# The last sixteen rows of a sum of reciprocals on one order list

## The chip, the cores and the metric

The kernel runs on one core of a Trainium2 chip. The metric is the device time of one execution in microseconds. The kernel before takes 172.44 us, the median of 12 runs (171.76 to 172.76).

## The reference

For x of 32 x 512 x 1024 float32, all positive, the output is the sum of 1/x over the last axis:

```python
def setup_inputs():
    batch, seq, dim = 32, 512, 1024
    return {"x": np.abs(np.random.randn(batch, seq, dim)).astype(np.float32) + 1e-6}

def reference(x):
    return np.sum(1.0 / x, axis=-1).astype(np.float32)
```

## The kernel before

The 16,384 sums are spread over 128 partitions, so each partition holds 128 rows ("row c" below is row c of all partitions at once) of 1024 elements. A ring of 40 rows in SBUF takes the loads; all are issued in row order on SP's queue (L124), eleven of 8 rows, six of 4 rows and eight of 2 rows. A load waits until the earlier users of its ring slots are done, and for the landing of the load eight before it, whose semaphore it takes.

Each row is cut into halves a and b of 512, and the kernel computes only one reciprocal for each pair of elements, in three steps:

- **Product** p = a * b. GpSimd (POOL) makes most of them (L143), two rows in one instruction where it can. For one row in a chunk of kind C, TensorE copies b to PSUM by a matmul with the identity (`add` into the tile `b`, L131) and VectorE multiplies a by it (L132).
- **Reciprocal** 1/p = exp(-ln p) on ScalarE (ACT): Ln in place with a scale of 2^17 (L154), then Exp with scale -1. For a chunk of kind A, Exp writes to a PSUM tile `r` (L162); for B and C it writes in place (L169).
- **Sum** on VectorE (DVE), `sum_row` (L93 to L104), which multiplies, and reduces to one column of `sums`. In a chunk of kind A each element of the row is multiplied by its r (a * 1/(ab) = 1/b, b * 1/(ab) = 1/a), 1024 elements. In B and C TensorE has added a + b into a PSUM tile `s` (L149, L150), and VectorE multiplies 512 elements of 1/p by s. Each sum is followed by a short read of the accumulator.

`LOADS` (L42 to L44) lists the chunks of two rows. The last sixteen rows, 112 to 127, are eight loads of one chunk each: A, B, A, C, A, B, A, C. In the last four rows (`SINGLE`, L34) Exp goes row by row, and the rest goes in pairs. The sums of a chunk are issued one chunk late (`waiting`, L152 and L170), so that VectorE doesn't stand before ScalarE.

Every engine works through its instructions in the program's order (`keep`). Tiles come from pools that rotate: four buffers for each of the two kinds of product tiles, three banks for s, one for b, two tiles of two banks for r. An instruction that takes a buffer waits until its former users are done.

Of the kernel before, what the change touches and what calls it, by code (L numbers as in the profile page):

```python
# [1 line left out]

# [6 lines left out]


@with_exitstack
def kernel(
    ctx: ExitStack,
    tc: tile.TileContext,
    x: bass.AP,
    out: bass.AP,
):

    nc = tc.nc
    f32 = mybir.dt.float32
    P = 128  # L30
    D = 1024
    H = D // 2
    F = 128
    SINGLE = 124  # L34

    R = 40

    S = float(2**17)

    A, B, C = (2, 0, 0), (2, 2, 0), (2, 2, 1)  # L42
    LOADS = [[A, B, A, B], [A, B, A, C]] * 5 + [[A, B, A, C]]
    LOADS += [[A, B], [A, C]] * 3 + [[A], [B], [A], [C]] * 2  # L44

    Ln = mybir.ActivationFunctionType.Ln
    Exp = mybir.ActivationFunctionType.Exp
    mult = mybir.AluOpType.mult
    plus = mybir.AluOpType.add

    x_v = x.flatten_outer_dims().rearrange("(p f) d -> p f d", p=P)
    out_v = out.flatten().rearrange("(p f) -> p f", p=P)

    act_sets = list(get_activation_tables(nc.m.arch).keys())
    nc.scalar.add_instruction(  # L55
        mybir.InstLoadActFuncSet(
            name=nc.get_next_instruction_name(),
            act_func_set_id=act_sets.index("natural_log_exp_and_others"),
            ins=[],
            outs=[],  # L60
        )
    )

    ppool = ctx.enter_context(tc.tile_pool(name="ppool", bufs=4))
    opool = ctx.enter_context(tc.tile_pool(name="opool", bufs=1))
    spool = ctx.enter_context(
        tc.tile_pool(name="spool", bufs=3, space=bass.MemoryType.PSUM)
    )
    bpool = ctx.enter_context(
        tc.tile_pool(name="bpool", bufs=1, space=bass.MemoryType.PSUM)  # L70
    )
    rpool = ctx.enter_context(
        tc.tile_pool(name="rpool", bufs=2, space=bass.MemoryType.PSUM)
    )

    ring = opool.tile([P, R, D], f32)
    sums = opool.tile([P, F], f32)
    ident = opool.tile([P, P], f32)
    make_identity(nc, ident)
    keep = tc.keep_in_program_order  # L80

    def add(bank, *halves):
        for k, half in enumerate(halves):
            i = nc.tensor.matmul(  # L84
                bank,
                lhsT=ident,
                rhs=half,
                start=k == 0,
                stop=k == len(halves) - 1,
            )  # L90
            keep(i)

    def sum_row(c, row, fac, out=None):  # L93
        i = nc.vector.tensor_tensor_reduce(  # L94
            out=row if out is None else out,
            in0=row,
            in1=fac,
            scale=S,
            scalar=0.0,
            op0=mult,  # L100
            op1=plus,
            accum_out=sums[:, c : c + 1],
        )
        keep(i)  # L104

    def sum_rows(c, xc, pr, sm, rc):
        m, e = xc.shape[1], len(sm)
        for j in range(e, m):
            row = xc[:, j, :].rearrange("p (h e) -> p h e", h=2)
            sum_row(  # L110
                c + j,
                row,
                rc[j - e].unsqueeze(1).to_broadcast([P, 2, H]),
                pr[:, e : e + 2, :] if j == e and e + 1 < m and c < SINGLE else None,
            )
        for j in reversed(range(e)):
            sum_row(c + j, pr[:, j, :], sm[j])

    waiting = None
    c0 = 0  # L120
    for chunks in LOADS:
        n = sum(m for m, _, _ in chunks)
        xt = ring[:, c0 % R : c0 % R + n, :]
        keep(nc.sync.dma_start(out=xt, in_=x_v[:, c0 : c0 + n, :]))  # L124

        made, q = [], 0
        for m, e, v in chunks:
            pr = ppool.tile([P, m, H], f32, tag="ps" if e else "pr")
            for j in range(v):
                b = bpool.tile([P, H], f32, tag="b")  # L130
                add(b, xt[:, q + j, H:])  # L131
                i = nc.vector.tensor_tensor(  # L132
                    out=pr[:, j, :], in0=xt[:, q + j, :H], in1=b, op=mult
                )
                keep(i)
            made.append(pr)
            q += m

        q = 0
        for (m, e, v), pr in zip(chunks, made):  # L140
            xc = xt[:, q : q + m, :]
            if v < m:
                i = nc.gpsimd.tensor_tensor(  # L143
                    out=pr[:, v:, :], in0=xc[:, v:, :H], in1=xc[:, v:, H:], op=mult
                )
                keep(i)
            sm = []
            for j in range(e):
                s = spool.tile([P, H], f32, tag="s")  # L149
                add(s, xc[:, j, :H], xc[:, j, H:])  # L150
                sm.append(s)
            if waiting:  # L152
                sum_rows(*waiting)
            keep(nc.scalar.activation(out=pr, in_=pr, func=Ln, scale=S))  # L154

            step = 1 if c0 + q >= SINGLE else m
            rc = []
            for j in range(e, m, step):
                to = min(j + step, m)
                r = rpool.tile([P, to - j, H], f32, tag="rc")  # L160
                keep(
                    nc.scalar.activation(  # L162
                        out=r, in_=pr[:, j:to, :], func=Exp, scale=-1.0
                    )
                )
                rc += [r[:, l, :] for l in range(to - j)]
            for to in range(e, 0, -step):
                r = pr[:, max(to - step, 0) : to, :]
                keep(nc.scalar.activation(out=r, in_=r, func=Exp, scale=-1.0))  # L169
            waiting = c0 + q, xc, pr, sm, rc  # L170
            q += m
        c0 += n
    assert c0 == F, c0
    sum_rows(*waiting)

    nc.sync.dma_start(out=out_v, in_=sums)


# [1 line left out]
_INS = ['x']  # L180
_OUTS = [((32, 512), 'float32')]


# [23 lines left out]
```

## Time and profile before

| | us |
|---|---|
| median of 12 runs | 172.44 |
| the profiled execution, its own time | 172.69 |
| its span, first to last instruction | 170.9 |
| POOL busy | 138.4 (81%) |
| ACT busy | 134.3 (79%) |
| PE busy | 131.6 (77%) |
| DVE busy | 122.4 (72%) |
| DMA, mean rate over the span | 393 GB/s |

The span runs from the first instruction to the last one of the profiled execution; the device time is a little more. The chain of work that ended last is found backwards from the last instruction: at each step to what released it. All times below that have a place ("at 161.95") are us from the start of the span. In the groups of instructions, the columns are the line, the engine, the operation, its output and inputs by tile name, partitions x elements, the count, and after the bar the busy time and mean duration in ns, and after the second bar the idle time ahead of them and what ended it. The granted TensorE clock is 0.999.

### The profile page before, as it was taken

To read this page: it belongs to the slowest core of one execution; us is meant where nothing else is said; L and a number is where in the kernel's file an instruction comes from. 1 tells how busy PE (TensorE), PEld (TensorE's weight loads), DVE (VectorE), ACT (ScalarE), POOL (GpSimd) and SP (SyncE) were. 2 spreads that over 40 slices of the span, in tenths; PEclk is the share of its full clock that TensorE was granted. 3 is DMA by queue.
4 is the path that set the end of the run, shared out by engine and by line. 5 is a ranking of instruction groups with operands and counts; after the bars stand their busy time and mean duration, and the time that the engine had idled before them with its cause. 6 is when DMAs were issued, how large, how long until landed. Compare 5 with 4: busy or idle time off the path is not lost.

```text
span 170.9 us, 1264 instructions
## 1 busy us (share of the span) xinstructions
PE 131.6 (77%) x278; PEld 50.1 (29%) x278; DVE 122.4 (72%) x267; ACT 134.3 (79%) x131; POOL 138.4 (81%) x70
## 2 busy tenths in 40 slices
PE   0008999594978879785988869788899999988790
PEld 0003333241322333232333323233243343333230
DVE  0000877748977677778777677888789898889783
ACT  3003979959797988978889787888999998998890
POOL 1008999499996999699996989989999999997920
PEclk9999999999999999999999999999999999999999
DMA  6999999899999999999999999999999999999400
GB/s 215 414 460 414 453 414 453 368 430 430 430 431 422 453 407 464 384 431 437 422 445 422 445 422 431 399 430 424 430 430 430 430 408 418 422 418 424 169 0 15
DMA packets 3751, 67.24 MB, mean 393 GB/s; under 512 B 417, under 2 KB 545, under 8 KB 545
## 3 DMA queue, kind: packets, MB, share of 16 engines
q1 hardware_dynamic: 3744, 67.18, 92.8%
q8 instruction: 2, 0.03, 0.1%
q14 instruction: 5, 0.03, 0.0%
HBM read 67.11 MB, written 0.07 MB: 393 GB/s over the span
## 4 chain that ended last, share of the span: by engine, by line
DMA 80%; POOL 7%; issue 3%; PE 3%; ACT 3%; DVE 2%; SPq 1%; DVEq 0%; POOLq 0%
DMA ring<-in_x_dram 80%; POOL pr L143 7%; PE s L84 2%; ACT pr L154 2%; DVE ring L94 1%; SPq L124 1%; DVE pr L94 1%; PE b L84 1%; ACT r L162 1%; DVEq L202 0%; ACT pr L169 0%; DVE sums L94 0%; POOLq L143 0%; DVEq L94 0%
## 5 line engine op out<-in xcount | busy, mean ns | idle before, releaser
L143 POOL TENSOR_TENSOR pr<-ring 128x1024 f32<-128x1024 f32 x64 | 137.7, 2184 | 24.4 <-DMA ring<-in_x_dram 24.1
L84 PE MATMUL s<-ring,ident 128*128 128x512 f32 x256 | 122.1, 613 | 32.9 <-DVE sums L94 16.9
L154 ACT ACTIVATE pr<-pr 128x1024 f32<-128x1024 f32 x64 | 67.4, 1053 | 29.3 <-POOL pr L143 29.2
L84 PEld LDWEIGHTS s<-ring,ident 128*128 128x128 f32 x256 | 46.5, 192 | 105.9 <-issue 62.5
L94 DVE CUSTOM_DVE_ANT_1 pr<-ring,r 128x1024 f32<-128x1024 f32 x31 | 37.9, 1221 | 44.9 <-ACT r L162 44.9
L94 DVE CUSTOM_DVE_ANT_0 pr<-pr,s 128x512 f32<-128x512 f32 x64 | 41.3, 683 | 0.7 <-PE s L84 0.5
L94 DVE CUSTOM_DVE_ANT_1 ring<-ring,r 128x1024 f32<-128x1024 f32 x33 | 40.1, 1216 | 0.0
L169 ACT ACTIVATE pr<-pr 128x1024 f32<-128x1024 f32 (+1 forms) x33 | 33.9, 1031 | 1.0
L162 ACT ACTIVATE r<-pr 128x1024 f32<-128x1024 f32 (+1 forms) x33 | 33.0, 1001 | 1.0
L84 PE MATMUL b<-ring,ident 128*128 128x512 f32 x22 | 12.0, 626 | 2.1 <-DMA ring<-in_x_dram 2.0
L94 DVE DVE_READ_ACCUMULATOR2_ANT sums<- 128x1 f32 x128 | 10.5, 82 | 0.0
L132 DVE TENSOR_TENSOR pr<-ring,b 128x512 f32<-128x512 f32 x11 | 7.5, 682 | 0.1
L84 PEld LDWEIGHTS b<-ring,ident 128*128 128x128 f32 x22 | 3.6, 188 | 9.7 <-DMA ring<-in_x_dram 8.3
L55 ACT ACT_TABLE_LOAD x1 | 1.3, 1283 | 0.7 <-PEq L191 0.7
masks.py:197 POOL MEMSET ident<- 128x128 f32 x1 | 0.2, 204 | 0.3 <-POOLq L191 0.3
masks.py:199 POOL TENSOR_SCALAR_AFFINE_SELECT ident<-ident 128x128 f32<-128x128 f32 x1 | 0.3, 292 | 0.1
L191 POOL MEMSET const-float32-0.0<- 128x1 f32 x1 | 0.1, 98 | 0.2 <-issue 0.2
L191 POOL MEMSET const-bfloat16-1.0<- 128x1 bf16 x1 | 0.1, 101 | 0.0
L191 POOL MEMSET const-uint8-127<- 128x1 uint8 x1 | 0.1, 101 | 0.0
L191 POOL MEMSET const-float32-1.0<- 128x1 f32 x1 | 0.1, 98 | 0.0
## 6 DMA issues: line engine op xcount, KB each, us to landing
ring<-in_x_dram SPq DMA_DIRECT2D x11, 4096.0 KB, 37.0
ring<-in_x_dram SPq DMA_DIRECT2D x6, 2048.0 KB, 37.3
ring<-in_x_dram SPq DMA_DIRECT2D x8, 1024.0 KB, 28.8
out_dram<-sums SPq DMA_DIRECT2D x1, 64.0 KB, 1.6
```

The costliest lines, as they stand in the source:

```text
L55: nc.scalar.add_instruction(mybir.InstLoadActFuncSet(name=nc.get_next_instruction_name(), act_func_set_id=act_sets.index("natural_log_exp_ ...
L84: i = nc.tensor.matmul(bank, lhsT=ident, rhs=half, start=k == 0, stop=k == len(halves) - 1,)
L94: i = nc.vector.tensor_tensor_reduce(out=row if out is None else out, in0=row, in1=fac, scale=S, scalar=0.0, op0=mult, op1=plus, accum_out ...
L124: keep(nc.sync.dma_start(out=xt, in_=x_v[:, c0 : c0 + n, :]))
L132: i = nc.vector.tensor_tensor(out=pr[:, j, :], in0=xt[:, q + j, :H], in1=b, op=mult)
L143: i = nc.gpsimd.tensor_tensor(out=pr[:, v:, :], in0=xc[:, v:, :H], in1=xc[:, v:, H:], op=mult)
L154: keep(nc.scalar.activation(out=pr, in_=pr, func=Ln, scale=S))
L162: nc.scalar.activation(out=r, in_=pr[:, j:to, :], func=Exp, scale=-1.0)
L169: keep(nc.scalar.activation(out=r, in_=r, func=Exp, scale=-1.0))
L191: nc = _bacc.Bacc("TRN2", target_bir_lowering=False, num_devices=1)
```

## The change

Rows 0 to 111 stay as they are. The chunks of the last sixteen rows leave `LOADS` (and `SINGLE` goes); their loads become six of two rows and four of one row. All their operations are written in one list, `ORDER`, and a new loop issues them as they stand there, so that each engine gets its share in that order. A letter is an operation, the number its row, and "+" means that it covers this row and the next:

- P: product on GpSimd. D: product on VectorE with both inputs in SBUF. B and V: TensorE copies b to PSUM, and VectorE multiplies by it.
- S: TensorE adds a + b into a tile s. L: Ln. E: Exp, in place for rows that have an S, else into a tile r. T: the sum on VectorE.
- W and X: row 124 goes another way: Ln over all 1024 elements of the row in place, then Exp with scale -1 and the sum over the row from ScalarE's accumulator straight into `sums`. This row has no product, no s and no work on VectorE.

VectorE's products are rows 117 (V) and 121 (D) where they were 118 and 126. The rows summed against s are 115, 118, 119, 122, 123, 126 and 127, where they were 114, 115, 118, 119, 122, 123, 126 and 127. Rows 125, 126 and 127 go through product, Ln, Exp and sum row by row. The store of `sums` now waits for ScalarE as well as for VectorE.

```diff
-    SINGLE = 124
...
-    LOADS += [[A, B], [A, C]] * 3 + [[A], [B], [A], [C]] * 2
+    LOADS += [[A, B], [A, C]] * 3
+    LAST = 112
+    LAST_LOADS = [2] * 6 + [1] * 4
+    ORDER = """
+        P112+ P114+ L112+ B117 E112+ P116 S115 V117 L114+ T113 L116+ P118 S118
+        T112 E114 E115 P119 T114 E116+ S119 P120 L118+ T115 D121 E118+ T117
+        L120+ S122 P122+ T116 E120+ T119 W124 T118 P125 L122+ T120 S123 P126
+        L125 T121 E122+ S126 P127 E125 T122 L126 T123 L127 S127 T125 E126 E127
+        T126 X124 T127
+    """
...
+    c0 = LAST
+    for n in LAST_LOADS:
+        xt = ring[:, c0 % R : c0 % R + n, :]
+        keep(nc.sync.dma_start(out=xt, in_=x_v[:, c0 : c0 + n, :]))
+        c0 += n
     assert c0 == F, c0
     sum_rows(*waiting)
+
+    prs, rs, ss, bs = {}, {}, {}, {}
+    order = ORDER.split()
+    added = {int(op[1:]) for op in order if op[0] == "S"}
+    dead = set()
+
+    def pair(c):
+        k = (c - LAST) // 2
+        if k not in prs:
+            pr = ppool.tile([P, 2, H], f32, tag=("pr", "ps")[k % 2])
+            prs[k] = pr
+        return prs[k]
+
+    for op in order:
+        kind, c, n = op[0], int(op[1:].rstrip("+")), 1 + op.endswith("+")
+        j = (c - LAST) % 2
+        rows = ring[:, c % R : c % R + n, :]
+        a, b = rows[:, :, :H], rows[:, :, H:]
+        pr = None if kind in "WX" else pair(c)[:, j : j + n, :]
+        if kind == "P":
+            keep(nc.gpsimd.tensor_tensor(out=pr, in0=a, in1=b, op=mult))
+        elif kind == "D":
+            keep(nc.vector.tensor_tensor(out=pr, in0=a, in1=b, op=mult))
+        elif kind == "B":
+            bb = bpool.tile([P, H], f32, tag="b")
+            add(bb, b[:, 0, :])
+            bs[c] = bb
+        elif kind == "V":
+            keep(
+                nc.vector.tensor_tensor(
+                    out=pr[:, 0, :], in0=a[:, 0, :], in1=bs[c], op=mult
+                )
+            )
+        elif kind == "S":
+            s = spool.tile([P, H], f32, tag="s")
+            add(s, a[:, 0, :], b[:, 0, :])
+            ss[c] = s
+        elif kind == "L":
+            keep(nc.scalar.activation(out=pr, in_=pr, func=Ln, scale=S))
+        elif kind == "E":
+            r = pr
+            if c not in added:
+                r = rpool.tile([P, n, H], f32, tag="rc")
+                rs.update({c + l: r[:, l, :] for l in range(n)})
+            keep(nc.scalar.activation(out=r, in_=pr, func=Exp, scale=-1.0))
+            if n == 2:
+                dead.add((c - LAST) // 2)
+        elif kind == "T" and c in added:
+            sum_row(c, pr[:, 0, :], ss[c])
+        elif kind == "T":
+            row = rows[:, 0, :].rearrange("p (h e) -> p h e", h=2)
+            k = (c - LAST) // 2
+            to = prs[k] if k in dead else None
+            dead.discard(k)
+            sum_row(c, row, rs[c].unsqueeze(1).to_broadcast([P, 2, H]), to)
+        elif kind == "W":
+            keep(nc.scalar.activation(out=rows, in_=rows, func=Ln))
+        elif kind == "X":
+            keep(
+                nc.scalar.activation(
+                    out=rows,
+                    in_=rows,
+                    func=Exp,
+                    scale=-1.0,
+                    accum_out=sums[:, c : c + 1],
+                )
+            )
 
     nc.sync.dma_start(out=out_v, in_=sums)
```

## The prediction

> **What bounds the kernel now.** I read the page's chain of work first, then that chain in order of time for the last 30 us, then the busy time by stretch, then the groups by shape of the last 24 us. The chain, as start us, us, what:
>
> ```profile
> 104.02 37.55 DMA ring<-in_x_dram
> ...
> 141.65 20.30 DMA ring<-in_x_dram
> 161.95 0.04 issue
> 161.99 1.13 PE b L84 x2
> 163.12 3.45 PE s L84 x8
> ...
> 167.40 0.60 DVE pr L94
> 168.00 0.01 DVE sums L94
> ```
>
> Until 161.95 the chain is loads and nothing else (the page gives them 80% of the span). From the last landing to the last sum it takes 168.01 - 161.95 = 6.06 us. In that tail it is not ScalarE but TensorE that is late: two b matmuls for row 126, then eight s matmuls for rows 126 and 127 in a row, and VectorE's last two sums behind them. After that come 2.9 us for the store and the end of the program (168.01 to 170.9), and 172.69 - 170.9 = 1.79 us outside the span. Only the tail of 6.06 us is open to an edit of the last rows.
>
> The stretches, each with us, busy time (count) of PE, PEld, DVE, ACT, POOL, then clock, DMA share, GB/s:
>
> ```profile
> 148.00:157.00 9.00, 7.72 (x17) 2.69 (x15) 8.48 (x20) 8.48 (x9) 7.87 (x4) 1.00 1.01 422
> 157.00:162.00 5.00, 3.68 (x9) 1.44 (x9) 3.82 (x9) 4.20 (x4) 4.78 (x3) 1.00 0.56 234
> 162.00:168.00 6.00, 4.55 (x10) 1.81 (x10) 5.41 (x13) 4.30 (x6) 1.29 (x2) 1.00 0.00 0
> ```
>
> The DMA engines are full to 157 and then run out unevenly. VectorE and ScalarE have 0.5 us of slack each in nine at 148 to 157, so a tail that gives ScalarE more work must find it there or after 157. In the tail VectorE is busy for 5.41 of 6.0 us.
>
> Prices of the tail's shapes (busy us, mean ns):
>
> ```profile
> L143 POOL TENSOR_TENSOR pr<-ring 128x1024 f32<-128x1024 f32 x6 | 14.2, 2379 | 1.4 <-DMA ring<-in_x_dram 1.1
> L154 ACT ACTIVATE pr<-pr 128x1024 f32<-128x1024 f32 x10 | 10.5, 1051 | 1.6 <-POOL pr L143 1.5 <-DVE pr L132 0.2
> L94 DVE CUSTOM_DVE_ANT_0 pr<-pr,s 128x512 f32<-128x512 f32 x12 | 7.8, 683 | 0.7 <-PE s L84 0.5 <-ACT pr L169 0.2
> L94 DVE CUSTOM_DVE_ANT_1 ring<-ring,r 128x1024 f32<-128x1024 f32 x6 | 7.2, 1216 | 0.0
> L162 ACT ACTIVATE r<-pr 128x1024 f32<-128x1024 f32 x4 | 4.1, 1028 | 0.1
> L143 POOL TENSOR_TENSOR pr<-ring 128x512 f32<-128x512 f32 x3 | 3.9, 1285 | 0.1
> L132 DVE TENSOR_TENSOR pr<-ring,b 128x512 f32<-128x512 f32 x2 | 1.4, 684 | 0.1
> L162 ACT ACTIVATE r<-pr 128x512 f32<-128x512 f32 x2 | 1.1, 592 | 0.0
> ```
>
> Queued, they follow each other closer than their means: in the trace POOL 2.33 and 1.24 us, ACT 0.97 (two rows) and 0.54 (one row), but 1.07 where an Exp waits for the Ln just before it; VectorE 1.14 (sum against r) and 0.61 (sum against s); TensorE 0.43 per matmul, so 1.72 per row of s. Hand-overs cost 0.03 us from POOL to ACT and from ACT to VectorE, 0.16 from TensorE's last matmul to VectorE (166.55 to 166.71).
>
> [...] The trace has 684 for L132. I take 0.69 for D121.
> [...]
>
> **The change part by part.** Up to row 111 every engine's order is the same. I take the state at hand-over from the trace: POOL free at 145.28, ScalarE ready for the Ln of rows 112-113 at 148.21, VectorE done with row 110 at 149.78. Loads land (last of 16 completions) at 144.60, 147.09, 149.57, 152.05, 154.54 and 157.02 for pairs 112 to 122, then 159.51 and 161.95 today.
>
> *Loads.* Two loads of two rows become four of one, in the same place of SP's queue. SP issues the last load today at 141.65, 20 us ahead of its landing; the new last one waits for rows 114-115 to land (147.09), still some 15 us ahead, so the queue doesn't run dry. A packet per partition took 1213, 614 and 312 ns at 32, 16 and 8 KB: by doubling, 10 to 15 ns of each are fixed. At 4 KB that is (312 + 10) / 2, some 160 ns (estimate), by eight per DMA engine 1.28 us a row. Rows land at 158.30, 159.58, 160.86 and 162.14: the last 0.2 later, the others sooner. Lower bound 1.24 a row (no fixed part), upper 1.5.
>
> *TensorE.* Removed: b of 118 and 126 and s of 114; added: b of 117, which stands ahead of S115 in its queue (S115 then runs 150.51 to 152.39, wanted at 154.79). Seven rows of s are left where there were eight. S127 needs the bank of row 122: T122 ends at 163.31, S127 runs 163.42 to 165.40. This replaces 166.55, a gain of 1.15 on the chain that ends last today.
>
> *POOL.* Six pairs and two single rows become three pairs (P112, P114, P122) and seven single rows: 118 and 126 come to POOL, 117, 121 and 124 leave it. A single row costs 1.24, half a pair 1.17. From 152.16: P118 to 153.44, P119 154.68, P120 155.93, P122 (landing 157.02) 157.13 to 159.51, P125 160.97, P126 162.25, P127 163.53 (today 163.39).
>
> *VectorE.* V117 waits for b (landing 149.57, two matmuls to 150.74): 150.77 to 151.45. T113, T112 to 153.73; T114, T115 to 155.48; D121 is ready at 155.41[...]: to 156.62. Behind it T117, T116, T119, T118, T120, T121 to 162.41; T122 to 163.31, T123, T125, T126 to 165.67, T127 from 165.59 (S127 ready 165.40 + 0.16, E127 at 165.28) to 166.28. In all one sum against s is gone (eight to seven; the eight against r stay, row 114's for row 124's), 0.61 less.
>
> *ScalarE.* 14 two-row and 4 one-row operations become 11 two-row and 8 one-row ones and W124 and X124: from 14 x 1.0 + 4 x 0.54 = 16.2 to 13 x 1.0 + 8 x 0.54 = 17.3, and the accumulator read. So it works longer, but nothing of VectorE has to follow its last instruction. By start: L112 148.21, E112 149.29, L114 150.25, L116 151.48 (0.25 idle for V117), E114 152.46, E115 153.00, E116 153.79 (0.25 idle: its r bank is free after T112), L118 154.76, E118 155.84, L120 156.80 (D121 done 156.62), E120 157.88, W124 158.84, L122 159.83 (P122 done 159.51), L125 161.00 (P125 done 160.97), E122 161.55, E125 162.51, L126 163.05, L127 163.59 (P127 done 163.53), E126 164.14, E127 164.67, X124 165.21. X124 takes 1.05, and then reads out its accumulator. No row here prices that read on ScalarE: it can't be below 0, and I bound it above by a whole 512-wide ACTIVATE, 0.6; I take 0.2, between VectorE's own read of 0.08 and that bound. It ends at 166.46.
>
> *Sum.* The last work ends at 166.46 (ScalarE; VectorE 166.28) in place of 168.01: 1.55 us less. The store now waits for ScalarE as well; the 2.9 us behind it stay. Against the profiled execution: 172.69 - 1.55 = 171.14. The median of the runs stands 0.25 below that execution: **170.9 us**.
>
> With the bounds: accumulator read 0 to 0.6 gives 166.28 to 166.86; 1.24 to 1.35 us a row gives 166.38 to 166.71; ScalarE 1.0 late at hand-over gives 166.75, VectorE 1.0 late gives no change. So 170.7 to 171.3 on the median, with 0.2 either way for the sampling.
>
> **The rivals.**
> - *The tail is landing-bound after all.* L127 starts when P127 is done, and my ScalarE queue reaches it only 0.03 later, so a later landing moves the end by its full size. At 1.5 us a row, row 127 lands at 163.02, the end is 167.31, the time 171.75. For it: row loads halve the packet, and the DMA engines end unevenly today. Against it: halving from 16 to 8 KB cost only some 2%.
> - *Slower: D121 misses its window.* POOL is idle only from 155.93 to 157.13, when P122 begins. If VectorE comes to D121 after 157.13[...] it waits until 159.51 and ends at 160.20. L120 then starts at 160.23 in place of 156.80, everything behind it on ScalarE follows without a gap, and X124 ends at 169.70: 1.69 later than today, 174.1. It decides from a delay of D121 of 1.7 us.[...] Against: VectorE's queue ahead of D121 is set by landings 5 us earlier.
> - *No change.* Several small new waits (E116 on T112, L116 on V117, S127 on T122) each 0.4 longer than drawn would bring the end to 166.46 + 1.2 = 167.7, 172.1. For it: all three stand in in-order queues, so what is behind waits too. Against: ScalarE makes up delays of its start to 1.0 us almost in full before L125, where POOL sets its time.
>
> **How the numbers follow.** Forecast (ScalarE's queue sets the end, 170.6 to 171.4): 0.68. Landing-bound (171.4 to 172.0): 0.18. No change (172.1 to 172.8): 0.08. Slower (D121): 0.06. About 0.2% is what a measurement of this kernel can tell from no change. Faster by over that: 0.68 + 0.18 = 0.86; within: 0.08; slower: 0.06. The range takes the forecast with its bounds and most of the landing case: 170.4 to 171.8.
>
> **What would show it.** Right: the chain's last pieces are ScalarE's X124 or VectorE's T127 near 166.4, no row of TensorE after 165.6, D121 within 155.4 to 156.7, ScalarE without a gap over 0.3 us from 148.2 on, POOL's last product ending near 163.5. Wrong: a wait of L120 for VectorE, P127 starting after 162.6, an accumulator read on ScalarE over 0.6, or main rows whose landings differ from today's by over 0.3.

## The result and the profile after

The changed kernel takes 170.43 us, the median of 11 runs (170.04 to 170.95), against 172.31 us for the kernel before, measured beside it. The ratio is 0.9894, 95% interval 0.9878 to 0.9910, so some 1.8 us or 1.1% faster (1.55 to 2.1 us). A second measurement gave 0.9893 (e10). The prediction was 170.9 us against 172.44, 1.55 us faster, with a range of 170.4 to 171.8.

The chain of work that ended last, in order of time, of the changed kernel (start us, us, what):

```profile
141.55 18.02 DMA ring<-in_x_dram
...
159.72 1.29 POOL pr L211
...
161.57 1.05 ACT pr L235
162.62 0.02 issue
162.64 0.50 DVE pr L108
...
163.94 1.13 DVE ring L108
...
165.69 0.60 DVE pr L108
166.29 0.01 DVE sums L108
```

The chain leaves the loads at 159.58, not at 161.95: what it follows is no longer the last landing but row 125's, whose product GpSimd makes at once. TensorE is gone from it; the two long pieces of s and b matmuls that closed the chain before have no successor here. The last work ends at 166.30 where it ended at 168.01. The span is 169.0 us.

The same stretches as before (us, then busy us and count of PE, PEld, DVE, ACT, POOL, clock, DMA share, GB/s):

```profile
148.00:157.00 9.00, 6.28 (x14) 2.52 (x14) 8.02 (x17) 8.42 (x11) 6.88 (x5) 1.00 1.00 413
157.00:162.00 5.00, 4.53 (x10) 1.92 (x11) 5.00 (x11) 4.77 (x6) 4.66 (x3) 1.00 0.61 242
162.00:168.00 6.00, 3.11 (x7) 0.87 (x5) 3.92 (x12) 4.25 (x8) 1.48 (x2) 1.00 0.04 11
```

From 157 to 162 VectorE is now busy all the time (5.00 of 5.00, before 3.82) and ScalarE nearly so (4.77, before 4.20). Work that used to come after 162 now runs before it: after 162 VectorE has 3.92 us left in place of 5.41, TensorE 3.11 in place of 4.55.

ScalarE from L120 on, where the predicted schedule can be held against it line by line:

```profile
156.81 1.04 ACT L229 ACTIVATE pr<-pr 128x1024 f32<-128x1024 f32 x1
157.88 1.03 ACT L235 ACTIVATE r<-pr 128x1024 f32<-128x1024 f32 x1
158.84 1.04 ACT L247 ACTIVATE ring<-ring 128x1024 f32<-128x1024 f32 x1
159.79 1.04 ACT L229 ACTIVATE pr<-pr 128x1024 f32<-128x1024 f32 x1
161.03 0.63 ACT L229 ACTIVATE pr<-pr 128x512 f32<-128x512 f32 x1 [0.20 <-POOL pr L211]
161.57 1.04 ACT L235 ACTIVATE pr<-pr 128x1024 f32<-128x1024 f32 x1
162.51 0.58 ACT L235 ACTIVATE r<-pr 128x512 f32<-128x512 f32 x1
163.03 1.13 ACT L229 ACTIVATE pr<-pr 128x512 f32<-128x512 f32 x2
164.07 1.13 ACT L235 ACTIVATE pr<-pr 128x512 f32<-128x512 f32 x2
165.11 1.04 ACT L250 ACTIVATE ring<-ring 128x1024 f32<-128x1024 f32 x1
166.06 0.19 ACT L250 ACTIVATION_READ_ACCUMULATOR ring<-ring 128x1 f32 x1
```

These are L120, E120, W124, L122, L125 (0.20 idle for GpSimd's product of row 125), E122, E125, L126 and L127, E126 and E127, X124 and its accumulator read. No start is more than 0.1 us from the predicted one.

Landings move from one profiled execution to the next by up to 1 us: GpSimd's product of rows 122 and 123, which follows their landing, starts at 157.18 in both kernels and at 156.19 in e8. So below I give for each kernel, beside the ratio, the time from the start of that product to the end of the last work. I call it the tail time. It is 168.01 - 157.18 = 10.83 us in the kernel before and 166.30 - 157.18 = 9.12 us in the changed one: 1.71 less.

### The profile page after: what moved, and what is told of

Same layout as the page of the kernel before. It is cut to its first block, busy times and chain, and to the rows that moved or that the text cites. A ratio compares the mean times of both kernels' runs of the same rounds, so it can differ in the third digit from the quotient of the medians.

```text
span 169.0 us, 1264 instructions
## 1 busy us (share of the span) xinstructions
PE 130.6 (77%) x272; PEld 50.2 (30%) x272; DVE 121.8 (72%) x265; ACT 134.7 (80%) x135; POOL 137.5 (81%) x72
## 4 chain that ended last, share of the span: by engine, by line
DMA 79%; POOL 8%; issue 4%; DVE 3%; ACT 3%; SPq 1%; POOLq 0%; DVEq 0%
DMA ring<-in_x_dram 79%; POOL pr L157 7%; DVE ring L108 2%; ACT pr L168 2%; DVE pr L108 1%; POOL pr L211 1%; SPq L138 1%; ACT r L173 1%; ACT pr L235 1%; DVE sums L108 0%; ACT pr L178 0%; POOLq L157 0%; DVEq L285 0%; POOLq L211 0%; ACT pr L229 0%
## 5 line engine op out<-in xcount | busy, mean ns | idle before, releaser
L157 POOL TENSOR_TENSOR pr<-ring 128x1024 f32<-128x1024 f32 (+1 forms) x56 | 121.1, 2198 | 22.9 <-DMA ring<-in_x_dram 22.9
L168 ACT ACTIVATE pr<-pr 128x1024 f32<-128x1024 f32 x56 | 59.0, 1053 | 28.2 <-POOL pr L157 28.2
L178 ACT ACTIVATE pr<-pr 128x1024 f32<-128x1024 f32 x28 | 29.6, 1058 | 0.9
L173 ACT ACTIVATE r<-pr 128x1024 f32<-128x1024 f32 x28 | 28.8, 1028 | 0.9
L211 POOL TENSOR_TENSOR pr<-ring 128x512 f32<-128x512 f32 (+1 forms) x10 | 15.8, 1605 | 2.5 <-DMA ring<-in_x_dram 2.5
L98 PE MATMUL b<-ring,ident 128*128 128x512 f32 x18 | 9.6, 616 | 0.3 <-DMA ring<-in_x_dram 0.3
L229 ACT ACTIVATE pr<-pr 128x1024 f32<-128x1024 f32 (+1 forms) x9 | 8.0, 902 | 0.5 <-DVE pr L220 0.3
L146 DVE TENSOR_TENSOR pr<-ring,b 128x512 f32<-128x512 f32 x9 | 6.2, 683 | 0.6 <-PE b L98 0.6
L235 ACT ACTIVATE r<-pr 128x1024 f32<-128x1024 f32 (+1 forms) x5 | 4.2, 850 | 0.2 <-DVE sums L108 0.2
L235 ACT ACTIVATE pr<-pr 128x512 f32<-128x512 f32 (+1 forms) x5 | 3.8, 786 | 0.0
L98 PE MATMUL bb<-ring,ident 128*128 128x512 f32 x2 | 1.1, 644 | 2.2 <-DMA ring<-in_x_dram 2.2
```

The source lines that it names most:

```text
L98: i = nc.tensor.matmul(bank, lhsT=ident, rhs=half, start=k == 0, stop=k == len(halves) - 1,)
L146: i = nc.vector.tensor_tensor(out=pr[:, j, :], in0=xt[:, q + j, :H], in1=b, op=mult)
L157: i = nc.gpsimd.tensor_tensor(out=pr[:, v:, :], in0=xc[:, v:, :H], in1=xc[:, v:, H:], op=mult)
L173: nc.scalar.activation(out=r, in_=pr[:, e:, :], func=Exp, scale=-1.0)
L211: keep(nc.gpsimd.tensor_tensor(out=pr, in0=a, in1=b, op=mult))
L235: keep(nc.scalar.activation(out=r, in_=pr, func=Exp, scale=-1.0))
```

## The experiments

Each experiment changes one part of the changed kernel (e4 of the kernel before). The order of the rest stays as near as it can, and for each variant one order was run. The edits show the lines that differ.

Theory: the tail is a set of in-order queues fed by landings, and each part of the change takes work off one of them at the time when it was late. Rivals: the gain is the removal of TensorE's late work alone; ScalarE's queue alone makes the end; single loads and single rows do nothing.

**e1: the last four rows loaded in pairs.**

```diff
-    LAST_LOADS = [2] * 6 + [1] * 4
+    LAST_LOADS = [2] * 8
```

> The changed kernel, but with the last four rows loaded as two loads of two rows, as before; every operation stays. My theory (the tail is a queue fed by landings): row 124 lands at 159.5 in place of 158.3 and row 126 at 161.95 in place of 160.8, so GpSimd's products of 126 and 127 move to 163.3 and 164.6, ScalarE's Ln of 127 to 164.6, and the last work ends near 167.4, 1.1 us later than in the changed kernel (166.3): some 171.5 us, ratio to before near 0.995. Rival (the gain is the removal of TensorE's and VectorE's late work, single loads do nothing): the end stays at 166.3 to 166.5, 170.4 to 170.6 us, ratio 0.989 to 0.990.

Measured: ratio 0.9959 (0.9944 to 0.9974), 171.13 us. The tail time is 10.19 us, 1.07 more than in the changed kernel. GpSimd in e1:

```profile
156.40 3.74 POOL L211 TENSOR_TENSOR pr<-ring 128x1024 f32<-128x1024 f32 x2 [1.22 <-DMA ring<-in_x_dram]
161.34 2.51 POOL L211 TENSOR_TENSOR pr<-ring 128x512 f32<-128x512 f32 x2 [1.20 <-ACT pr L229]
```

The products of 122, 123 and 125 run in one go, then GpSimd stands for 1.20 us, until the pair with row 126 has landed. (The view names ScalarE for that idle time. But the instruction waits on a load as well: the pair landed at 161.18, and GpSimd's wait for it ended at 161.20; that ScalarE finished an instruction at 161.33 is a coincidence.) In the changed kernel the products of 125, 126 and 127 follow each other without a gap (159.71 to 163.48). Single loads are worth 1.1 us in this order, as the theory had it; the rival falls.

**e2: row 124 the common way.**

```diff
-        L120+ S122 P122+ T116 E120+ T119 W124 T118 P125 L122+ T120 S123 P126
-        L125 T121 E122+ S126 P127 E125 T122 L126 T123 L127 S127 T125 E126 E127
-        T126 X124 T127
+        L120+ S122 P122+ T116 E120+ T119 P124 T118 P125 L122+ L124 T120 S123
+        P126 L125 T121 E122+ S126 P127 E124 E125 T122 L126 T123 L127 S127 T124
+        T125 E126 E127 T126 T127
```

> The changed kernel, but row 124 goes the common way (product on GpSimd, Ln and Exp over 512, sum on VectorE against r) in place of Ln, Exp and sum over 1024 on ScalarE. My theory: ScalarE has 1 us less to do, but GpSimd's products of 125, 126 and 127 each move by 1.2 (the last to 164.45) and VectorE has one sum of 1.14 more in the last stretch, where it has no gap; the last work ends near 168.4, VectorE's, 2.1 us later than in the changed kernel, so nothing of the gain is left: 172.5 us, ratio 1.001. Rival (ScalarE's queue is what ends the changed kernel, the other engines have room): 1 us less on ScalarE gives an end at or before 166.3, at most 170.4 us, ratio at most 0.989.

Measured: ratio 1.0017 (1.0010 to 1.0023), 172.07 us; tail time 11.28 us, 2.16 more. VectorE's last stretch, up to its idle time and from the sum of row 124 on:

```profile
160.25 1.21 DVE L108 CUSTOM_DVE_ANT_1 ring<-ring,r 128x1024 f32<-128x1024 f32 x1
...
162.84 0.69 DVE L108 CUSTOM_DVE_ANT_0 pr<-pr,s 128x512 f32<-128x512 f32 x1 [1.38 <-ACT pr L235]
...
164.06 1.22 DVE L108 CUSTOM_DVE_ANT_1 ring<-ring,r 128x1024 f32<-128x1024 f32 x1
...
165.21 1.22 DVE L108 CUSTOM_DVE_ANT_1 ring<-ring,r 128x1024 f32<-128x1024 f32 x1
...
166.96 0.68 DVE L108 CUSTOM_DVE_ANT_0 pr<-pr,s 128x512 f32<-128x512 f32 x1
```

The same wait in the changed kernel:

```profile
162.64 0.69 DVE L108 CUSTOM_DVE_ANT_0 pr<-pr,s 128x512 f32<-128x512 f32 x1 [0.38 <-ACT pr L235]
```

From the wait on, VectorE makes the sums of 122 and 123, then two of 1.14 (rows 124 and 125) and then those of 126 and 127 without a gap, while ScalarE has been done since 165.93. With this one row off ScalarE the whole gain is gone, and a little more. So ScalarE's queue alone doesn't make the end: the 2 us that it spends on row 124 save GpSimd a product and VectorE a sum.

The 2.16 us are two things. One sum more is 1.14. The other 1.0 is VectorE's longer wait, 1.38 in place of 0.38, so the "no gap" of the expectation did not hold. VectorE waits there for the Exp of rows 122 and 123, and that stands on ScalarE behind the Ln of row 125, which waits for GpSimd's product of 125, now 1.2 us later. This second part belongs to the order: with that Exp ahead of the Ln of 124 and 125 it might be avoided. That order was not run, so 2.16 is what row 124's way is worth in this order and not in the best one.

**e3: rows 126 and 127 as a pair.**

```diff
-        L120+ S122 P122+ T116 E120+ T119 W124 T118 P125 L122+ T120 S123 P126
-        L125 T121 E122+ S126 P127 E125 T122 L126 T123 L127 S127 T125 E126 E127
-        T126 X124 T127
+        L120+ S122 P122+ T116 E120+ T119 W124 T118 P125 L122+ T120 S123 P126+
+        L125 T121 E122+ S126 E125 T122 X124 L126+ T123 S127 T125 E126+ T126
+        T127
```

> The changed kernel, but rows 126 and 127 go through product, Ln and Exp as a pair (row 124's Exp moves ahead of them on ScalarE to fill the wait). My theory: the product of the pair ends at 164.5, the Ln at 165.6, the Exp at 166.7, and two sums follow, end near 168.0, 1.7 us later than in the changed kernel: 172.1 us, ratio 0.999. Rival (two instructions for one cost their fixed part twice, and the row-by-row form gains nothing): end at or before 166.3, ratio at most 0.989.

Measured: ratio 0.9995 (0.9986 to 1.0003), 171.76 us; tail time 10.92 us, 1.80 more. The chain:

```profile
161.26 2.41 POOLq L285
163.67 0.02 issue
163.69 1.07 ACT pr L229
164.76 0.02 issue
164.78 1.07 ACT pr L235
165.84 0.02 issue
165.87 0.69 DVE pr L108
```

From the landing one step stands behind the other, each two rows long: the product (2.37 in the trace, under the name of GpSimd's queue here), Ln, Exp, and then two sums. Row by row, the step of one row runs beside the next step of the row ahead of it (in the changed kernel GpSimd's product of row 127, 162.21 to 163.48, beside the Ln of row 126 from 163.03). Since e1, e2 and e3 all keep TensorE's relief and lose from 1.1 us to the whole gain, the rival that this relief alone is the gain falls.

**e4: the kernel before with one edit**, row 126's product on GpSimd in a pair with 127, no copy of b.

```diff
-    LOADS += [[A, B], [A, C]] * 3 + [[A], [B], [A], [C]] * 2
+    LOADS += [[A, B], [A, C]] * 3 + [[A], [B], [A], [C], [A], [B], [A], [B]]
```

> The kernel before, with one edit: the product of row 126 goes from VectorE (and its copy of b from TensorE) to GpSimd, as a pair with row 127. My theory (in the kernel before TensorE's chain ends last, and the copy of b stands at its head): TensorE's sums of halves start 0.86 earlier and end at 165.7, but the pair's product ends at 164.5, so that Ln, two Exps and two sums end near 167.45 in place of 168.0: 171.8 us, ratio 0.997. Rival (TensorE is not late in any way that counts): no gain or a loss, ratio 1.000 to 1.006, since the product on GpSimd comes 1.1 us later.

Measured: ratio 0.9958 (0.9942 to 0.9975), 171.14 us; tail time 10.35 us, 0.48 less than in the kernel before (expected 0.55). In the kernel before VectorE waited 0.47 us for TensorE's last matmul of row 127 (to 166.71); here TensorE ends at 164.98 and that wait is gone. So TensorE's lateness counted, and one line takes it away. The edit takes VectorE's product of row 126 (0.69) away as well, and the run doesn't tell the two apart. It then stops: Ln of the pair waits for the pair's product to 163.7, the Exp of row 127 ends at 165.45, and VectorE, without a gap since 163.11, is free for its sum at 165.47. Two queues come to the last sums at the same time.

**e5 and e6: VectorE's product of row 121 put where it meets GpSimd's product of 122 and 123.** In e5 as D (both inputs in SBUF), in e6 as V (b copied to PSUM).

```diff
-        T112 E114 E115 P119 T114 E116+ S119 P120 L118+ T115 D121 E118+ T117
-        L120+ S122 P122+ T116 E120+ T119 W124 T118 P125 L122+ T120 S123 P126
+        T112 E114 E115 P119 T114 E116+ S119 P120 L118+ T115 E118+ T117 S122
+        P122+ T116 D121 L120+ E120+ T119 W124 T118 P125 L122+ T120 S123 P126
```

(e6 has `P120 B121 S119` for `S119 P120` as well, and `V121` for `D121`.)

> The changed kernel, but VectorE's product of row 121 (both inputs in SBUF) stands behind the sums of rows 117 and 116 in its queue, so that it comes up near 157.6, just after GpSimd has begun the 2.37 us product of rows 122 and 123 (157.2 to 159.55). This is the slower rival of the prediction made on purpose. If VectorE's instruction waits for the whole of GpSimd's (as the 1.10 us of this product in the changed kernel suggest): it ends near 160.05, ScalarE's Ln of 120 starts at 160.1 in place of 156.8, and the last work ends near 169.45: 173.6 us, ratio 1.007. If it is only slowed to about 1.1 us: it ends at 158.7, the last work ends near 168.1, 172.2 us, ratio 0.999. If there is no contention at all (0.69): as e6, 167.7, 171.85 us, ratio 0.997.

> As e5, but VectorE takes b of row 121 from PSUM, where TensorE has copied it (as for row 117), so that only one of its inputs is in SBUF. Place in the queue as in e5. My theory: no contention, 0.69 us, ends at 158.3; the Ln of 120 starts at 158.4, the last work ends near 167.75: 171.9 us, ratio 0.9975. Rival (the place in the queue alone makes the cost[...]): like e5, within 0.2 us of it.

Measured: e5 1.0095 (1.0067 to 1.0124), tail time 12.18 us, 3.06 more than the changed kernel; e6 0.9980 (0.9973 to 0.9987), 10.49 us, 1.37 more. The product, in e5:

```profile
156.85 2.38 DVE L213 TENSOR_TENSOR pr<-ring 128x512 f32<-128x512 f32 x1
```

and in e6, at the same moment:

```profile
156.85 0.68 DVE L220 TENSOR_TENSOR pr<-ring,bb 128x512 f32<-128x512 f32 x1
```

GpSimd's product in e5:

```profile
156.35 2.34 POOL L211 TENSOR_TENSOR pr<-ring 128x1024 f32<-128x1024 f32 x1 [1.21 <-DMA ring<-in_x_dram]
```

The trace shows no wait ahead of VectorE's instruction: the wait is inside its duration. It is issued 0.50 us after GpSimd began, and ends 0.55 after GpSimd's end (158.69, then 159.24), while GpSimd's own product takes no longer than elsewhere (2.34, in the changed kernel 2.38). ScalarE's L120 stood for 3.24 us behind it. So of the 3.06 us, 1.37 are the place in the queue (e6) and 1.69 the longer product (2.38 in place of 0.68). The slower rival of the prediction is real, and near the price that was put on it (169.70 against the forecast's 166.46, so 3.24 us); the changed kernel is clear of it by 1.8 us of VectorE's queue (155.38 against 157.18).

**e7: row 121 as V in the changed kernel's place** (`P120 B121 S119` and `V121`).

> The changed kernel, but VectorE takes b of row 121 from PSUM (TensorE copies it, ahead of the s of row 119), in the changed kernel's place of the queue. My theory: the product takes 0.69 in place of 1.10 but must wait for the copy (155.7), so it ends at 156.4 as it did (156.48); no change, last work at 166.3, 170.4 us, ratio 0.989. Rival (the contention of the product costs time at the end): up to 0.4 us earlier, 170.0 us, ratio 0.987.

Measured: ratio 0.9903 (0.9887 to 0.9919); tail time 9.12 us, the same as the changed kernel. The product took 0.69 in place of 1.10, but VectorE first waited 0.33 us for the copy.

**e8: row 117 as D** (`B117` left out, `D117` for `V117`).

> The changed kernel, but row 117's product on VectorE has both inputs in SBUF, without TensorE's copy of b. It comes up at 149.7, as GpSimd begins the 1.27 us product of row 116 (149.86 in the changed kernel). My theory: [...]in either order the product of 117 is done by 151.7 and that of 116 by 151.9, ScalarE's Ln of 116 starts at 151.2 to 151.9 (151.53 in the changed kernel), and this is taken up by ScalarE's later wait for the product of 125: no change at the end, 166.3, 170.4 us, ratio 0.989. Rival (the wait of Ln 116 for VectorE's product is on the path that sets the end): 0.3 us earlier or later, ratio 0.987 or 0.991.

Measured: ratio 0.9895 (0.9879 to 0.9911); tail time 9.23 us. The product of row 117 ended 0.55 us after GpSimd's product of 114 and 115 (149.53, then 150.08). GpSimd's next product, of row 116, began at 149.49, before VectorE's had ended, and took 1.73 us where the others of its kind take 1.28. ScalarE's L116 started 0.03 us after that product's end (151.22, then 151.25), and the tail time grew by 0.11, which the ratio can't tell from nothing.

**e9: ScalarE's idle time taken out by order**, and **e10: the changed kernel again**, measured together.

```diff
-        P112+ P114+ L112+ B117 E112+ P116 S115 V117 L114+ T113 L116+ P118 S118
-        T112 E114 E115 P119 T114 E116+ S119 P120 L118+ T115 D121 E118+ T117
+        P112+ P114+ L112+ B117 E112+ P116 S115 L114+ T113 V117 E114 E115 P118
+        S118 T112 L116+ P119 T114 E116+ S119 P120 L118+ T115 D121 E118+ T117
...
-        L125 T121 E122+ S126 P127 E125 T122 L126 T123 L127 S127 T125 E126 E127
+        E122+ T121 L125 S126 P127 E125 T122 L126 T123 L127 S127 T125 E126 E127
```

> The changed kernel with ScalarE's two idle stretches taken out by order alone: Exp of 114 and 115 before Ln of 116, the sum of 113 before VectorE's product of 117, and Exp of 122 before Ln of 125. My theory (from row 125 on GpSimd is without a gap and its last product, at 163.45, sets when ScalarE can finish): ScalarE's idle time goes, but the Ln of 127 starts at 163.5 all the same, and the last work ends 0.0 to 0.15 us earlier than in the changed kernel: not to be told from it, ratio 0.988 to 0.9895. Rival (ScalarE's idle time ahead of row 125, some 0.7 us, is what the end is made of): 0.5 us or more earlier, ratio at most 0.987.

> The changed kernel itself, unchanged, beside e9: the measure of what two measurements of one kernel differ by. Ratio 0.988 to 0.991; last work at 166.2 to 166.4, and 2.7 to 2.9 us from there to the end of the span.

Measured: e9 0.9900 (0.9885 to 0.9914), tail time 9.22 us; e10 0.9893 (0.9877 to 0.9910), 9.12 us. No gain, as expected, but not for the reason given. The trace of e9 shows no wait of ScalarE at all from 148 to the end, and its L127 began 0.22 us after the product of row 127 (162.73, then 162.95): in that execution it was ScalarE's own unbroken queue that held it, not GpSimd. The new order also puts the Exp of rows 114, 122 and 125 right behind their own Ln, where it starts some 0.1 us later than it would behind another row's (1.07 us after the start of a two-row Ln, not 0.97), so it gives back part of what it takes out. In e10 ScalarE's only wait is this:

```profile
ACT pr L229 <- POOL pr L211: 0.2, 1, 0.2
```

In this execution ScalarE began the Ln of 112 only 8.45 us ahead of GpSimd's product of 122; in the first profile of the same kernel it was 9.06, so it starts 0.6 us later here. The two waits ahead of row 125, 0.52 us together in the first profile, are gone here without any edit, and yet the tail time is the same 9.12. So it is e10 beside the first profile, more than e9, that speaks against the rival: this idle time is slack. ScalarE's queue and GpSimd's last product lie within about 0.2 us of each other, and taking idle time from one gains nothing. None of the versions tried can be told from the changed kernel as better.

## Why the prediction was right

- *What bounds.* "Only the tail of 6.06 us is open": held. The loads end at the same pace, and the tail shrinks.
- *Loads.* Packets of 4 KB took 161 ns (160 estimated), and rows 124 to 127 landed at 158.31, 159.58, 160.81 and 162.04 (predicted 158.30 to 162.14). The landing-bound rival's 1.5 us a row didn't occur; e1 shows that landings do move the end: row 126 landed 1.15 us later, counted from the product of 122, and the end came 1.07 later.
- *TensorE.* S127 ran 163.39 to 165.37 (predicted 163.42 to 165.40).
- *POOL.* Its last product ended at 163.48 (predicted 163.53).
- *VectorE.* D121 ended at 156.48, not 156.62: I let it wait for GpSimd's end and then take its whole 0.69, and what remains after that end is 0.55. It had no effect at the end, since VectorE waits for E122 at 162.6 in the drawn schedule and in the trace. That it waits for GpSimd at all was my assumption, which no trace of the kernel before showed; at one place in the queue the runs gave 0.68 with one SBUF input (e6) and 2.38 with two (e5).
- *ScalarE.* Mis-sized by 0.21 in two small terms. I took 0.2 after X124 for the accumulator read; it takes 0.19, but begins 0.09 before X124 ends, so it adds 0.1. And the last single rows follow each other at 0.52 and not 0.54, so X124 starts at 165.11 and not 165.21. The hand-over came 0.09 earlier than drawn (148.12 against 148.21), which the wait for row 117's product took up at once (0.33 where 0.25 was drawn). So ScalarE ended at 166.25 (predicted 166.46), and VectorE (166.30, predicted 166.28) was last, not ScalarE. W124 and X124 took 1.04 each, within the 1.03 to 1.06 of the two-row operations before, which have as many elements.
- *Sum.* The end came at 166.30, not 166.46, 0.16 more gain. From there to the end of the span it was 2.68 us, where I kept the 2.9 of the profiled execution before. In the ten experiments it was 2.57 to 2.77, in e4, whose program is that of before but for one row, 2.58; so the 2.9 looks like a property of that one execution, though the kernel before was profiled only once. These two make the difference between 1.55 and the 1.9 us by which the spans differ. Outside the span it went the other way: 1.79 us before, 1.95 after, so the profiled executions' own times differ by 172.69 - 170.95 = 1.74.
- *The range.* The median of 170.43 lies only 0.03 us inside the range, and below the 170.7 to 171.3 that the bounds of the mechanism gave and the 170.6 to 171.4 of the forecast. About 0.2 of the miss is in the terms above. Most of the rest is sampling: I put the median 0.25 below the profiled execution, as before, and the profiled execution after happened to lie 0.52 above its median. That the absolute time fell inside the range is in part luck; the ratio, which compares runs made side by side, is the better witness. Its interval, 1.55 to 2.1 us, has the predicted 1.55 at its edge and the 1.71 of the traces inside.
- *The rivals.* No change: the new waits (L116 on VectorE 0.33, E116 on VectorE 0.19, L125 on GpSimd 0.20) came out within 0.1 us of what was drawn, and e10, where the first two are missing and the tail time is the same, shows that they cost nothing. The 0.33 is a little over the 0.3 us that the prediction allowed a gap on ScalarE. Slower: e5 gives it where VectorE comes late.

One thing the prediction did not say: the gain doesn't divide among the parts. Undoing single loads gives back 1.1 us (e1), pairing the last rows 1.8 (e3), sending row 124 the common way 2.2 (e2), in sum far more than the 1.7 of the whole change, because each part relieves another queue and a queue that isn't relieved ends the tail. The sizes belong to these orders. In e2 1.0 of the 2.2 is a wait that another order might avoid. In e1 ScalarE's X124 is last (166.59, VectorE 166.37) although ScalarE stood idle for 0.56 us ahead of the Ln of 127, where X124 might have gone.

## What to carry to other kernels

When loads bound a kernel, write the tail down engine by engine from the last landings, with the durations and hand-overs of the trace: here such a schedule gave the end of the changed kernel within 0.2 us, and the ends of nine variants, drawn with the changed kernel's trace at hand and counted from one landing, within 0.25. Cut the last loads and the last steps into single rows so that steps of different rows overlap (undone, they cost 1.07 us in e1 and 1.80 in e3), and move work to an engine that has slack there even where it costs more (row 124 takes 2 us of ScalarE where the common way takes 1.1, and saves 1.2 us of GpSimd and 1.1 us of VectorE). Judge each part by undoing it, and look in the trace whether the loss comes from that part or from an order that no longer fits: engines that end within 0.2 us of each other hide what the next edit is worth.

## What the runs showed of the hardware

- A VectorE product with two SBUF inputs that met a GpSimd product ended 0.55 us after GpSimd's end in each of these three cases (row 121 in the changed kernel: 155.93, 156.48; in e5: 158.69, 159.24; row 117 in e8: 149.53, 150.08). In the trace the wait counts as VectorE's busy time: 0.75 to 2.38 us, where the same product with b in PSUM takes 0.69 (0.68 in e6). No run shows the two-input form without a GpSimd product beside it.
- GpSimd's next product took longer as well: 1.73 us in place of 1.28 in e8 (row 116), 1.49 in place of 1.28 in e5 (row 125).
- ScalarE's accumulator read takes 187 ns, of which about half lies under the ACTIVATE before it (in the changed kernel 166.06 to 166.25, X124 until 166.15).
